# A wait ahead of the position-bias loads of the second attention

## The chip, the cores and the metric

The kernel runs on one core of a Trainium2 chip. The metric is the time of one execution on the device in microseconds. The median of three runs before the change is 2534.94 us (2533.12 to 2541.66).

## The reference

One layer of an encoder is applied to two groups of 2048 tokens (prompt and sample) of width 1024, all in float32. From the normalised input one projection gives queries, keys, values and gates of two attentions. The first attention looks at a window of 128 tokens to either side. The second looks at a neighbourhood: the 2048 tokens are a grid of 32 rows by 64 columns, and each token sees 8 rows by 16 columns around it. Both results are gated, go through one output projection and are added to the input, and a last gated term is added. What matters here is the second attention (cut):

```python
sc = jnp.einsum('bnqhd,banchd->bnhqac', qr, kb).astype(jnp.float32) * scale
drow = rs + jnp.arange(wr) - r + NA_ROWS_MAX - 1
bias = rpb_cols[:, drow].transpose(2, 0, 3, 1, 4)
sc = jnp.where(mask, sc + bias.astype(jnp.float32), -jnp.inf)
...
pr = jax.nn.softmax(sc, axis=-1)
...
o = jnp.einsum('bnqhac,banchd->bnqhd', pr, vb)
```

The bias depends on a head and on where a key lies relative to its query. The kernel reads it, with the mask folded in, from a table in HBM.

## The kernel before, in words

The program has three stages. In the first (up to about 760 us) the first attention runs, in the second (about 760 to 1905 us) the second one, and in the third (from 1905 us) the output projection and the last gate. The change is in the second stage.

The second attention is cut into 64 units, `unit_b(f)`: two halves of the heads, two groups of tokens, and 16 blocks of 8 rows by 16 columns (b counts the four blocks of rows, cb the four of columns, cb fastest). A unit has 128 queries and four heads. Its keys are a window of 12 or 15 grid rows by 24 or 32 columns, so that a head's scores are 128 x 288, 384, 360 or 480. The steps of a unit are:

- `sc(h)`: two matrix products per head make the scores (scb); DVE adds the bias and takes the maximum (`softmax`, L277), and behind the fourth head DVE makes the negative maxima (L288).
- `exps`: ACT makes four exponentials (L294), heads 0, 2, 1, 3 in this order. All but the last units also turn the probabilities into another order: four copies `tn<-s` from one place in SBUF to another, issued by ACT as DMAs between and behind the exponentials (L301). They are pinned to their places in ACT's order.
- `load_values`: SP loads the values (`vw<-v_d`, L891) in three or four pieces into rotating buffers that become free with the products of the unit before.
- `pt(x)`: TensorE transposes a head's copied probabilities (ptb, L262), ACT and DVE split the result into two parts (L923, L924).
- `po(x)`: TensorE multiplies them with the values (pob), and `fin` gates and stores the result (ob_d, L952).

The bias of a unit is loaded by SP (L879) into one of two halves of a buffer `bt[0]`; a unit with cb = 2 has the same table as the one with cb = 1 before it and loads none, so there are 48 loads for 64 units. The load stands in the program at the start of its own unit. It may start as soon as its half of the buffer is free.

The order of TensorE's work is written out: `PLAN_B` says at which share of a unit's time each step is traced, and between the steps the projection of a later unit (pqk and pvg, five to six units ahead) fills TensorE. All its instructions are chained in that order. The other engines' and SP's queues are ordered by a planner, which simulates the program and issues what is ready, earlier instructions of the program first; `P(...)` and `behind(...)` pin single instructions. Within a queue instructions then run strictly in that order. SP's queue in this stage also carries the stores of values (v_d, L837), the loads of the next input (stx, L352), reloads of weights (wa and wb, L197 and L1001) at the two places where the set of weights changes, and loads and stores for later stages.

Of the kernel before, what the change touches and what calls it, by code (L numbers as in the profile page):

```python
# [42 lines left out]
def row_type(b):  # L43
    return (0, 1, 1, 2)[b]


def col_type(cb):
    return (0, 1, 1, 2)[cb]
# [57 lines left out]
def emit(ctx, tc, io):  # L106
    nc = tc.nc
# [37 lines left out]
    copies = []  # L145
# [105 lines left out]
    def behind(ins, other=None):  # L251

        tc.add_manual_dep(ins.ins, (other or last_pe[-1]).name,
                          mybir.DependencyInfo(mybir.DependencyClass.NoSync, mybir.DependencyReason.DATA),
                          reason="behind the product")
# [25 lines left out]
    def sm_tiles():  # L281
        return {"s": [], **{k: ap.tile([128, 4], F32, tag=k, name=k, bufs=3) for k in ("mx", "nm", "den", "rd")}}

    def exps(sm, fct, gs, sink=None, turned=None):

        mx, nm, den, rd, ss = (sm[k] for k in ("mx", "nm", "den", "rd", "s"))
        if sink is None:
            nc.vector.tensor_scalar_mul(nm, mx, -1.0)  # L288
            yield
        else:  # L290
            nc.vector.scalar_tensor_tensor(out=nm, in0=mx, scalar=-1.0, in1=sink[1], op0=ALU.mult, op1=ALU.min)  # L291
        waiting = []
        for n_, i in enumerate((0, 2, 1, 3) if sink is None else range(4)):
            ex = nc.scalar.activation(ss[i], ss[i], AF.Exp, bias=nm[:, i:i + 1], accum_out=den[:, i:i + 1])  # L294
            if sink is None and (n_ == 0 or turned is not None):
                P(ex)
            if sink is None and turned is not None:
                waiting.append(i)
                for k in waiting[:1] if n_ in (1, 2) else waiting[:] if n_ == 3 else ():
                    to = turned[:, k, :ss[k].shape[-1]]  # L300
                    P(nc.scalar.dma_start(to.bitcast(F32), ss[k]))  # L301
                    ss[k] = to
                    waiting.remove(k)
        if sink is not None:
            es = ap.tile([128, 4], F32, tag="es", name="es", bufs=3)
            nc.vector.tensor_tensor(out=es, in0=sink[0], in1=nm, op=ALU.add)
            nc.scalar.activation(es, es, AF.Exp)
            yield
            behind(nc.vector.tensor_tensor(out=den, in0=den, in1=es, op=ALU.add))
            nc.vector.reciprocal(out=nm, in_=den)  # L310
            nc.gpsimd.tensor_copy(rd, nm)
            nc.gpsimd.tensor_copy(rd[0:64, 1::2], nm[64:128, 0::2])
            nc.gpsimd.tensor_copy(rd[64:128, 0::2], nm[0:64, 1::2])
        else:
            nc.vector.reciprocal(out=rd, in_=den)
        nc.gpsimd.tensor_scalar_mul(rd, rd, fct)
        g2 = ap.tile([128, 4, HD], F32, tag="g2", name="g2", bufs=2)
        nc.gpsimd.tensor_tensor(out=g2, in0=gs.rearrange("p (h d) -> p h d", h=4),
                                in1=rd.unsqueeze(2).broadcast_to([128, 4, HD]), op=ALU.mult)
        sm["g2"] = g2.rearrange("p h d -> p (h d)")  # L320
        yield
# [70 lines left out]
    def big(shape, dt, name):  # L392
        return ap.tile(shape, dt, tag="big", name=name, bufs=3)
# [287 lines left out]
    def unit_a(f, kv):  # L681
# [6 lines left out]
        def sc(i):  # L688
            pair, half = divmod(i, 2)
            a, z = span[half]  # L690
            c0, n = 128 * t - 128 + 64 * half, z - a
            if half == 0:
                if not s2:
                    s2.extend([ap.tile([128, 3, 640], F32, tag="ev", name="s2", bufs=1), 0])
                pairs.append(s2[0][:, s2[1] % 3])
                s2[1] += 1
                if not right:
                    nc.gpsimd.memset(pairs[pair][:, 256:320], 0.0)
            ps = ptile([128, 512], "sc", "sc")
            for j, q in enumerate(qs[f]):  # L700
                mm(ps[:, :n], q[kv][:, 128 * i:128 * i + 128], ks_a[:, kv, c0 + a:c0 + z], j == 0, j == 1)
            softmax(i, ps, n, mask[:, a:z], sm, pairs[pair][:, 320 * half + a:320 * half + z])
            if i == 3:
                got["ex"] = exps(sm, y[:, 11:12], gs[:, 256 * kv:256 * kv + 256],
                                 (snk[:, 0, 4 * kv:4 * kv + 4], snk[:, 1, 4 * kv:4 * kv + 4]))
                next(got["ex"])
# [156 lines left out]
    bt = []  # L863

    def unit_b(f):
        half, st = divmod(f - 2 * NT, 2 * NT)
# [6 lines left out]
        n = nr * ncol  # L873
        if cb != 2:
            off, _ = BIAS_OFF[(row_type(b), col_type(cb))]
            if not bt:
                bt.append(big([128, 2, 4, 512], F32, "bias"))
            bt.append(bt[0][:, len(bt) % 2])
            nc.sync.dma_start(bt[-1][:, :, :n], io["bias"][half][:, off:off + 4 * n].rearrange("p (h n) -> p h n", h=4))  # L879
        bias = bt[-1]  # L880
        vw = []

# [18 lines left out]
        def sc(h):  # L901
            ps = ptile([128, 512], "sc", "scb")
            for j, q in enumerate(qs[f]):
                mm(ps[:, :n].rearrange("p (r c) -> p r c", c=ncol), q[h % 2][:, 128 * (h // 2):128 * (h // 2) + 128],
                   ks_b[h % 2][:, r0:r0 + nr, h // 2, c0:c0 + ncol], j == 0, j == 1)
            softmax(h, ps, n, bias[:, h, :n], sm)
            if h == 3:
                if not tn:
                    tn.append(ap.tile([128, 4, 480], F32R, tag="ev", name="tn", bufs=1))
                got["ex"] = exps(sm, hr_b[:, st:st + 1], gs, turned=tn[0] if f < 6 * NT - AHEAD - 1 else None)  # L910
                next(got["ex"])
# [204 lines left out]
    for f in range(6 * NT):  # L1116
# [8 lines left out]
        for kv in range(2 if in_a else 1):  # L1125
            unit = unit_a(f, kv) if in_a else unit_b(f)
            for part, now, act, i in PLAN_A if in_a else PLAN_B:
                at = (kv + part) / (2 if in_a else 1)
                while spent < at * total:
                    spent += next(stream, total)  # L1130
                if now or prev:
                    (unit if now else prev)[act](i)
            prev = unit
# [18 lines left out]
    with tc.tile_pool(name="c", bufs=1, reuse_waits="tile") as op:  # L1152
# [208 lines left out]
        for m in range(7 * len(groups)):  # L1361
            n, i = divmod(m, 7)
# [94 lines left out]
```

## Time and profile before

| what | value |
|---|---|
| median of three runs | 2534.94 us (2533.12 to 2541.66) |
| the profiled execution's own time | 2547.61 us |
| its span, first to last instruction | 2545.8 us |
| TensorE (PE) busy | 2469.8 us, 97% |
| VectorE (DVE) busy | 1704.6 us, 67% |
| ScalarE (ACT) busy | 1413.7 us, 56% |
| GpSimd (POOL) busy | 851.1 us, 33% |
| mean granted TensorE clock | 0.989 |
| loads of the bias (L879) | 48, of 576 to 960 KB |
| copies tn<-s (L301) | 232, of 144 to 240 KB |

PE is TensorE's matrix products, PEld its weight loads, DVE VectorE, ACT ScalarE, POOL GpSimd, SP SyncE. ACTq and SPq are the sequencers of ACT and SP, which issue DMAs. A row of a timeline gives start, duration, engine, line, operation and the names of the tiles (out<-in), with the number of merged instructions; in brackets stands the idle time of the engine before it and what ended that. A row of the windows view gives the stretch, its length, the busy time and number of instructions of each engine (PE, PEld, DVE, ACT, POOL), the granted clock of TensorE as a share of full speed, the busy share of the DMA engines and GB/s. A row of waits gives who waited for whom: us in total, number of times, longest.

### The profile page before, as it was taken

The page shows a single profiled execution, that of the slowest core. Times are in us where ns is not written, and L with a number is a line of the kernel's source. Part 1 is how long each engine was busy: PE and PEld are TensorE (multiplying, and loading weights), DVE is VectorE, ACT ScalarE, POOL GpSimd, SP SyncE. Part 2 cuts the span into 40 slices and gives each one's busy share as a digit, 9 for nine tenths or more (in the row PEclk, how much of TensorE's full clock was granted, in tenths as well). Part 3 has the DMA queues.
Part 4 walks back from the last instruction along what each step waited for, and adds up shares of the span by engine and source line. Part 5 has one row for each costly group of instructions (what it writes and reads, how often), then busy time and mean ns, then how long its engine had stood idle before and what let it go on. Part 6 is the DMA issues. An engine that isn't in the chain of part 4 may idle for free. (4 is left out here: it accounts for less than half of the span.)

```text
span 2545.8 us, 40929 instructions
## 1 busy us (share of the span) xinstructions
PE 2469.8 (97%) x13062; PEld 2073.9 (81%) x13062; DVE 1704.6 (67%) x4215; ACT 1413.7 (56%) x3408; POOL 851.1 (33%) x1363
## 2 busy tenths in 40 slices
PE   8999999999999999999999999999899999999999
PEld 7888888888888777887777777877778888888887
DVE  6877777777765665666566666665545665777776
ACT  5777777767664555565555555665664222344443
POOL 4555555555443544444444333433110000000000
PEclk9999999999999999999999999999999999999999
DMA  6423323232445766666977676776968555656665
GB/s 206 133 92 98 96 92 100 90 100 92 137 139 176 232 211 213 221 228 202 336 228 220 192 240 225 233 242 218 334 205 298 166 182 178 230 181 238 226 227 172
DMA packets 279288, 485.55 MB, mean 191 GB/s; under 512 B 31617, under 2 KB 120097, under 8 KB 274849
## 3 DMA queue, kind: packets, MB, share of 16 engines
q1 hardware_dynamic: 245376, 437.84, 52.6%
q10 hardware_dynamic: 33696, 45.09, 5.0%
q8 instruction: 104, 1.70, 0.3%
q14 instruction: 112, 0.91, 0.1%
HBM read 307.72 MB, written 134.23 MB: 174 GB/s over the span
## 5 line engine op out<-in xcount | busy, mean ns | idle before, releaser
L258 PE MATMUL pqk<-wa,xr 128*128 128x512 f32 x1536 | 464.2, 420 | 0.0
L258 PE MATMUL pvg<-wb,xr 128*128 128x512 f32 x1536 | 449.0, 405 | 0.0
L294 ACT ACTIVATE s<-s,nm 128x320 f32<-128x320 f32 (+6 forms) x512 | 293.4, 574 | 131.7 <-DVE nm L291 118.8
L258 PEld LDWEIGHTS pvg<-wb,xr 128*128 128x128 f32 x1536 | 271.8, 189 | 33.6
L258 PEld LDWEIGHTS pqk<-wa,xr 128*128 128x128 f32 x1536 | 263.6, 193 | 30.3
L370 POOL TENSOR_TENSOR xr<-stx,xr 128x512 fp32r<-128x512 f32 x186 | 238.2, 1292 | 136.2 <-ACT xr L369 103.2
L1242 ACT CAST opd<-raw 128x512 fp32r<-128x512 f32 x224 | 131.5, 618 | 270.6 <-PE acca L1260 117.9
L1243 DVE TENSOR_TENSOR opd<-raw,opd 128x512 fp32r<-128x512 f32 x224 | 146.7, 688 | 145.3 <-ACT opd L1242 145.3
L258 PE MATMUL pg<-wb,xr 128*128 128x512 f32 x768 | 233.1, 410 | 1.0 <-DVE vv L527 1.0
L258 PE MATMUL pq<-wa,xr 128*128 128x512 f32 x768 | 219.4, 400 | 0.0
L924 DVE TENSOR_TENSOR p_t<-ptb,p_t 128x368 fp32r<-128x368 f32 (+5 forms) x256 | 122.8, 488 | 135.7 <-ACT p_t L923 133.9
L942 ACT COPY otb<-pob 64x512 f32<-64x512 f32 x128 | 74.3, 581 | 209.2 <-PE pob L258 208.9
L923 ACT CAST p_t<-ptb 128x368 fp32r<-128x368 f32 (+5 forms) x256 | 107.6, 426 | 138.4 <-PE ptb L262 127.4
L1260 PE MATMUL accc<-opd,wb 128*128 128x512 f32 x768 | 176.7, 390 | 0.0
L1260 PE MATMUL acca<-opd,wa 128*128 128x512 f32 (+1 forms) x780 | 175.9, 386 | 0.5 <-ACT r L1338 0.5
L1260 PE MATMUL acca<-opd,s 128*128 128x512 f32 x768 | 175.4, 390 | 0.0
L143 POOL TENSOR_TENSOR yb<-vrb,power 128x8 f32<-128x8 f32 x64 | 106.4, 1662 | 200.0 <-DVE vrb L804 196.0
L1260 PEld LDWEIGHTS acca<-opd,wa 128*128 128x128 f32 x780 | 145.1, 188 | 30.1 <-ACT r L1338 0.7
L1260 PEld LDWEIGHTS accc<-opd,wb 128*128 128x128 f32 x768 | 144.3, 188 | 29.8
L1260 PEld LDWEIGHTS acca<-opd,s 128*128 128x128 f32 x768 | 144.2, 188 | 29.8
L262 PEld LDWEIGHTS ptb<-rowwise,tn 128*128 128x128 f32 (+2 forms) x756 | 86.6, 140 | 98.6 <-DMA tn<-s 63.9
L258 PEld LDWEIGHTS pob<-p_t,vw 128*128 128x128 f32 (+2 forms) x832 | 135.8, 193 | 27.3 <-DVE p_t L924 7.6
(174 smaller groups left out, 5244.2 us busy)
## 6 DMA issues: line engine op xcount, KB each, us to landing
stx<-x_b SPq DMA_DIRECT2D x128, 256.0 KB
vw<-v_d SPq DMA_DIRECT2D x96, 256.0 KB
stx<-x_a SPq DMA_DIRECT2D x64, 256.0 KB
stn<-x_n SPq DMA_DIRECT2D x64, 256.0 KB
v_d<-vb SPq DMA_DIRECT2D x64, 256.0 KB
ple_d<-ev SPq DMA_DIRECT2D x64, 256.0 KB
xres<-x_r SPq DMA_DIRECT2D x64, 256.0 KB
x_d<-r SPq DMA_DIRECT2D x64, 256.0 KB
```

The costliest lines, as they stand in the source:

```text
L143: nc.gpsimd.tensor_tensor(out=y, in0=v, in1=power.broadcast_to([128, n]), op=ALU.pow)
L258: pinned(nc.tensor.matmul(out, lhsT, rhs, start=start, stop=stop))
L262: pinned(nc.tensor.transpose(out.bitcast(F32R), in_, eye))
L294: ex = nc.scalar.activation(ss[i], ss[i], AF.Exp, bias=nm[:, i:i + 1], accum_out=den[:, i:i + 1])
L370: low.tensor_tensor(out=lo, in0=raw, in1=hi.bitcast(F32), op=ALU.subtract)
L923: nc.scalar.copy(hi, pf)
L924: nc.vector.tensor_tensor(out=lo, in0=pf, in1=hi.bitcast(F32), op=ALU.subtract)
L942: nc.scalar.copy(ot[a:a + 64], pq[z:z + 64])
L1242: P(nc.scalar.copy(hi, v))
L1243: P(nc.vector.tensor_tensor(out=lo, in0=v, in1=hi.bitcast(F32), op=ALU.subtract))
L1260: pinned(nc.tensor.matmul(ps[:, cols], w[k][:, a, c:c + 128], o[:, b, cols], start=i in (0, 1, 4) and k == 0 and j == 0, stop=k == 3 and j ...
```

## The change

The kernel keeps a note of the last exponential of the second attention that was traced, `last_ex`. Each load of a bias gets a dependency on the instruction noted there when the load is traced: SP waits with the load until that exponential has finished. `after` is the helper that enters the dependency. The copies, the exponentials and the sizes of all transfers stay as they are.

```diff
+    last_ex = []
+
+    def after(ins, other):
+
+        tc.add_manual_dep(ins.ins, other.name, mybir.DependencyInfo(mybir.DependencyClass.Sync, mybir.DependencyReason.DATA),
+                          reason="behind the copies")
+
...
             ex = nc.scalar.activation(ss[i], ss[i], AF.Exp, bias=nm[:, i:i + 1], accum_out=den[:, i:i + 1])
+            if sink is None:
+                last_ex[:] = [ex.ins]
...
-            nc.sync.dma_start(bt[-1][:, :, :n], io["bias"][half][:, off:off + 4 * n].rearrange("p (h n) -> p h n", h=4))
+            load = nc.sync.dma_start(bt[-1][:, :, :n],
+                                     io["bias"][half][:, off:off + 4 * n].rearrange("p (h n) -> p h n", h=4))
+            if last_ex:
+                after(load, last_ex[0])
```

## The prediction

> **What bounds the kernel now.** I read the page first, then the waits of the stretch in which the second attention runs, then busy times unit by unit, then the queues.
>
> ```profile
> span 2545.8 us, 40929 instructions
> PE 2469.8 (97%) x13062; PEld 2073.9 (81%) x13062; DVE 1704.6 (67%) x4215; ACT 1413.7 (56%) x3408; POOL 851.1 (33%) x1363
> ```
>
> TensorE (PE) is busy for 97% of the span, so only its idle 76 us and its slow stretches can be won. The waits from 807 to 1800 us (who waited for whom: us in total, times, longest), the last two rows from other queues:
>
> ```profile
> PE ptb L262 <- DMA tn<-s: 44.9, 46, 2.8
> PE pob L258 <- DVE p_t L924: 2.3, 5, 0.9
> ACT q1b L857 <- DMA bias<-bias: 6.9, 3, 2.3
> SPq L879 <- DVE nm L288: 60.3, 14, 6.3
> ```
>
> PE's one large wait is for the copies tn<-s, by which the exponentials of a unit get into the order that its transposes (ptb) read. Now stretches of the windows view, each from a unit's first exponential to the next one's: length, then the busy times of PE, PEld, DVE, ACT, POOL, then PE's granted clock. The first and third units (cb=1) have no bias load in them; the second and fourth, the next ones (cb=2) with the same shapes, have one:
>
> ```profile
> 1035.25:1051.13 15.88, 15.88 (x88) 13.24 (x87) 10.49 (x27) 9.66 (x23) 7.94 (x9) 1.00 0.70 232
> 1051.13:1067.69 16.56, 15.52 (x88) 12.86 (x87) 10.37 (x27) 9.71 (x23) 6.67 (x8) 1.00 0.76 251
> 1166.84:1183.67 16.83, 16.83 (x96) 14.15 (x95) 11.24 (x27) 9.96 (x23) 7.93 (x9) 1.00 0.52 165
> 1183.67:1201.98 18.31, 16.78 (x96) 13.83 (x95) 10.74 (x27) 10.15 (x23) 7.98 (x9) 1.00 0.81 263
> ```
>
> Without a load PE is never idle; with one the unit is 0.7 to 1.5 us longer, all of it idle PE. The reason stands in the queues. SP's timeline, ACT's, then PE's, for those first two units and the one before them:
>
> ```profile
> 1018.75 0.38 SPq L879 DMA_DIRECT2D bias<-bias  x1
> 1019.22 0.93 SPq L891 DMA_DIRECT2D vw<-v_d  x2
> ...
> 1034.46 1.28 SPq L891 DMA_DIRECT2D vw<-v_d  x3
> ...
> 1050.35 1.28 SPq L891 DMA_DIRECT2D vw<-v_d  x3
> 1051.72 0.38 SPq L879 DMA_DIRECT2D bias<-bias  x1
> ```
>
> ```profile
> 1035.99 0.47 ACTq L301 DMA_DIRECT2D tn<-s  x1
> ...
> 1051.87 0.47 ACTq L301 DMA_DIRECT2D tn<-s  x1
> ...
> 1053.05 0.62 ACT L294 ACTIVATE s<-s,nm 128x384 f32<-128x384 f32 x1
> ...
> 1053.80 1.22 ACTq L301 DMA_DIRECT2D tn<-s  x1
> ```
>
> ```profile
> 1025.31 0.35 PE L262 MATMUL ptb<-rowwise,tn 128*96 128x128 f32 x3
> ...
> 1041.00 0.45 PE L262 MATMUL ptb<-rowwise,tn 128*128 128x128 f32 x3
> ...
> 1044.02 0.46 PE L258 MATMUL pob<-p_t,vw 128*128 128x256 f32 x3
> 1044.83 0.38 PE L262 MATMUL ptb<-rowwise,tn 128*128 128x128 f32 x3
> ...
> 1058.02 0.45 PE L262 MATMUL ptb<-rowwise,tn 128*128 128x128 f32 x3 [1.04 <-DMA tn<-s]
> ```
>
> In the unit without a load the first copy is issued at 1035.99 and PE reads it at 1041.00, 5.0 us later, without waiting. In the next one a bias load goes out 0.15 us ahead of the first copy (1051.72, 1051.87), and the copy is there after 6.15 us: PE stood for 1.04. In the unit before both the load went out at 1018.75, well ahead of the exponentials, and the first transposes at 1025.31 waited for nothing. So the load hurts when it starts among the copies. Their sizes, of the units with 384 and 480 columns and of the load shared by most:
>
> ```profile
> tn<-s ACTq DMA_DIRECT2D x60, 240.0 KB
> bias<-bias SPq DMA_DIRECT2D x16, 720.0 KB
> ...
> tn<-s ACTq DMA_DIRECT2D x56, 192.0 KB
> ```
>
> The stall has a second price. After many of these stalls the granted clock is 0.50 for 3.4 us. Ten such stretches lie in units with a load and a stall (the first and the last are shown, then the 3.4 us just ahead of the one at 992.0, and the whole stage):
>
> ```profile
> 937.40:940.80 3.40, 3.40 (x13) 2.71 (x13) 0.92 (x2) 1.05 (x3) 1.73 (x2) 0.50 0.71 237
> ...
> 1749.80:1753.20 3.40, 3.40 (x15) 2.86 (x14) 0.54 (x1) 0.98 (x2) 2.12 (x2) 0.50 0.27 77
> 988.60:992.00 3.40, 1.92 (x12) 1.45 (x13) 1.75 (x4) 1.95 (x5) 0.40 (x1) 1.00 1.08 383
> ...
> 810.77:1799.61 988.84, 938.06 (x5040) 772.05 (x5038) 618.70 (x1562) 567.72 (x1335) 422.74 (x491) 0.98 0.71 230
> ```
>
> **The change part by part.** No instruction goes or comes but a semaphore wait ahead of 47 of the 48 bias loads (the first has no exponential before it). What is waited for is more than it seems. A load is traced when its own unit begins, and the exponential then on record is the fourth of the unit before. Today a load goes out as soon as its half of the double buffer is free, that is behind the last softmax of the unit that read it (the 60.3 us in which SP stands at L879 for DVE nm), one to three units ahead of use. Afterwards it goes out one unit ahead, behind that unit's fourth exponential: in the second unit shown at about 1053.05 + 0.62, near 1053.8 in place of 1051.72, 2.1 us later, and level with the fourth copy.
>
> *Stalls at ptb, 44.9 us.* The copies' first three are then issued 0.7 to 1.9 us ahead of the load, as in a unit with none. The fourth goes out beside it, 1053.80 - 1051.13 = 2.65 us behind the first exponential. Taking for it the 6.15 us of the copy that had a load 0.15 us ahead, it lands at 2.65 + 6.15 = 8.8, and PE asks for it at 1044.83 - 1035.25 = 9.6: covered by 0.8 us. So the units with a load become like those without. Bounds: all 44.9 gone, or 20 left if the fourth copy misses by half a us in most units. I take 40, near the upper end, since the row without a load (PE busy 15.88 of 15.88) is the nearest case; the rest is kept for stalls that have another cause.
>
> *Clock.* Ten stretches at half clock cost 10 x 3.4 x 0.5 = 17 us; the whole stage's row says 988.84 x (1 - 0.98) = 20. Each lies in a unit whose stall is 1.5 us or longer. I take 17; bounds 8 (if half the stalls stay) and 20.
>
> *ACT's wait on a landing.* In units whose load leads, ACT stood up to 2.3 us at its fourth copy until the bias had landed (6.9 in 3 waits), and PE behind that 2.3 us at pob. With the load behind the copies this goes: 1 us, bounds 0 and 2.3.
>
> *A load that comes too late.* DVE adds the bias to a unit's four score products. The rows that tell how long a load takes, when it is needed, and SP's queue where weights are reloaded (one piece of the chain of waits, DVE's and SP's timeline):
>
> ```profile
> 1620.30 5.08 DMA bias<-bias
> 1047.90 0.55 DVE L277 CUSTOM_DVE_ANT_0 s<-scb,bias 128x384 f32<-128x384 f32 x1
> ...
> 1221.57 5.86 SPq L197 DMA_DIRECT2D wa<-sp_1wa  x5
> 1227.66 1.87 SPq L891 DMA_DIRECT2D vw<-v_d  x2
> 1229.58 0.43 SPq L879 DMA_DIRECT2D bias<-bias  x1
> ...
> 1234.88 0.64 DVE L277 CUSTOM_DVE_ANT_0 s<-scb,bias 128x480 f32<-128x480 f32 x1
> 1786.03 0.44 SPq L879 DMA_DIRECT2D bias<-bias  x1
> ...
> 1789.89 0.64 DVE L277 CUSTOM_DVE_ANT_0 s<-scb,bias 128x480 f32<-128x480 f32 x1
> ```
>
> In an ordinary unit a load issued at 2.65 behind the first exponential is needed at 1047.90 - 1035.25 = 12.65, 10.0 us later, and takes 5.08 in a quiet case; beside copies I estimate 7.5 (the 6.15 of a 192 KB copy and some 500 KB more at the 383 GB/s of the window at 988.60). It is hidden, with 2.5 us to spare. Not so at the two reloads of weights: the load at 1229.58 is not for the softmax at 1234.88 but two units on; the load for that softmax was issued a unit earlier. It will now queue with the weights in SP, most likely at that same place, and land 5.08 to 7.5 us later: 0 to 2.2 us late; at 1786.03, 1.2 to 3.6 us late. If it is put ahead of the weights it costs nothing. Bounds 0 and 5.8; I take 4, near the upper end, since the weights share its way.
>
> *The wait itself* holds SP from the load's turn to the exponential. Behind it stand the store of ob_d, then v_d and the next x, which go out 1.5 us and more later anyway; ACT, DVE and PE execute nothing more.
>
> Sum: 40 + 17 + 1 - 4 = 54 us. Against the profiled execution's own 2547.6 (span 2545.8) that gives 2493.6. That execution is 12.7 us above the median of the runs shown, 2534.94. The last 640 us are free of such waits, so the surplus probably lies in these same stalls; then a timed run has only 54 - 12.7 = 41 to win. Between 41 and 54 I take 48: **2487 us**.
>
> **The rivals.**
>
> *The collision only moves.* The load still goes out level with the fourth copy and 0.65 us behind the third. For it: the 0.8 us of cover is thin, and wider units have copies of 240 KB instead of 192, so 6.15 may be 7.7 there. If half the units with a load lose 1 us at their last transposes and half the slow clock stays, 54 falls by 21 + 8.5 to 25: 2510 us. Against: PE asks for the four copies 1.1 to 1.5 us apart (1041.00 to 1044.83), and they are issued 0.65 apart, so each later copy has more room.
>
> [...]
>
> *The clock stays slow.* If something else than these stalls halves the clock, the 17 us stay: 2504. For it: the window 988.60 to 992.00 ahead of a slow one was no idle one, PE was busy in 1.92 of its 3.40 us. Against: all ten lie in units with a long stall.
>
> [...]
>
> *SP stands in the way (slower).* If the planner leaves the load ahead of the value loads vw, as at 1018.75 and 1019.22 now, these wait for the fourth exponential too. vw would go from 1050.35 to 1053.8 and behind 720 KB, 3.4 + 2 us later. Without that, vw issued by 1035.74 is used by pob at 1044.02, 8.3 us later, of which it needs 5.08 to 7.5; so a unit would lose 2.2 to 4.6, say 3.4 us. It decides from 17 units on (17 x 3.4 = 58, what the rest wins); in all 42 it makes 2535 - 48 + 143 = 2630, in half of them 2558. Against: today's lead comes where the softmax ends before vw's buffer is free; the fourth exponential ends 3 us later, when at 1050.35 vw has been issued in the common order.
>
> *Given back elsewhere (no change).* The bytes stay, and the DMA engines are busy 0.71 of the stage. 2 us later the load meets v_d's store and the next x, whose split PE needs. If that stall is as long, 2535. Against: the unit of 1166.84 has room (0.52), and x is issued late in a unit for the next but one.
>
> **How the numbers follow.** Forecast 0.60, clock stays slow 0.05, collision moved 0.15, no change 0.09, SP in the way 0.11. About 0.3% (7.6 us) is what a measurement of this kernel can tell from no change: faster 0.60 + 0.05 + 0.15 = 0.80, same 0.09, slower 0.11. The forecast's own range: 44.9 + 20 + 2.3 = 67 less nothing gives 2468; 20 less of stalls and 9 less of clock leaves 25, 2510. The range that leaves out the slower case and most of no change is 2468 to 2520.
>
> **What would show it.** Right: PE's wait at ptb for tn<-s falls from 44.9 to below 8; the clock of the stage is 1.00; outside the reloads every bias load starts 2.4 to 3.5 us behind its unit's first exponential; units of 1051.13's and 1183.67's kind take 15.9 and 16.8. DVE waits for the bias at the two reloads, by up to 5.8 us together. Wrong: pob waiting for vw (SP in the way), waits at the third and fourth ptb of a unit (collision moved), DVE waiting for the bias in ordinary units, or PE waiting for xr.

## The result and the profile after

The changed kernel takes 2491.13 us (median of four runs, 2490.16 to 2493.02) where the one before takes 2536.16 us (2533.12 to 2541.66) beside it: a ratio of 0.9821, with a 95% interval of 0.9802 to 0.9840. That is 45 us faster. The forecast was 2487 us and 48 us. The change shifts the line numbers: the exponentials are L301 now, the copies L310, the loads of the bias L888, the loads of the values L903, the store of ob_d L964.

The head of the page:

```profile
span 2490.3 us, 40934 instructions
...
PE 2447.5 (98%) x13062; PEld 2060.5 (83%) x13062; DVE 1705.6 (68%) x4215; ACT 1412.8 (57%) x3408; POOL 853.1 (34%) x1363
```

The span is 55.5 us shorter than that of the profiled execution before. TensorE's idle time, the span less its busy time, went from 2545.8 - 2469.8 = 76.0 to 42.8 us: 33 us. Its busy time for the same 13062 products went from 2469.8 to 2447.5: 22 us, which is mostly the clock (its mean went from 0.989 to 0.998, and 0.009 of 2500 us is 23). The waits of the stage (from 807 us to the last copies):

```profile
PE ptb L262 <- DMA tn<-s: 15.8, 18, 3.1
...
PE scb L258 <- DVE mx L277: 3.6, 2, 2.5
DVE s L277 <- DMA bias<-bias: 3.0, 2, 2.1
...
PE pob L258 <- DVE p_t L936: 0.4, 2, 0.2
```

TensorE's wait for the copies fell from 44.9 to 15.8 us. ACT's wait for a bias to land (6.9 us) has no row left. New are the two rows in the middle: VectorE waits for a bias, and TensorE behind it. Now the four kinds of units that the prediction showed, two without a load and, behind each, one with a load and the same shapes; then the whole stage, one reload of weights and the stretch at half clock within it:

```profile
1020.34:1035.96 15.62, 15.62 (x88) 13.25 (x87) 10.50 (x27) 9.77 (x23) 7.96 (x9) 1.00 0.71 236
1035.96:1051.28 15.32, 15.32 (x88) 12.89 (x87) 10.10 (x27) 9.64 (x24) 6.71 (x8) 1.00 0.85 271
1145.52:1162.32 16.80, 16.80 (x96) 14.13 (x95) 11.27 (x27) 9.97 (x24) 7.96 (x9) 1.00 0.53 165
1162.32:1179.44 17.12, 16.56 (x96) 13.88 (x95) 10.84 (x27) 9.97 (x24) 7.98 (x9) 1.00 0.87 280
810.07:1768.00 957.93, 935.74 (x5137) 777.46 (x5136) 630.81 (x1589) 580.58 (x1367) 426.82 (x498) 1.00 0.76 245
1196.54:1218.73 22.19, 18.04 (x88) 14.43 (x87) 11.05 (x27) 9.86 (x24) 7.89 (x9) 0.92 0.92 307
1205.50:1208.90 3.40, 3.40 (x13) 2.72 (x13) 1.68 (x4) 1.89 (x4) 2.91 (x2) 0.50 1.00 352
```

The narrow unit with a load took 16.56 us before and takes 15.32 now, with no idle TensorE. The wide one (480 columns) went from 18.31 to 17.12 and still holds 0.56 us of idle time, a wait for a copy at its first transposes:

```profile
1168.72 0.54 PE L262 MATMUL ptb<-rowwise,tn 128*128 128x128 f32 x4 [0.56 <-DMA tn<-s]
```

The queues of the narrow unit, SP, ACT, then the transposes on TensorE:

```profile
1035.18 1.28 SPq L903 DMA_DIRECT2D vw<-v_d  x3
1037.96 0.37 SPq L964 DMA_DIRECT2D ob_d<-o_tb  x1
1038.61 0.38 SPq L888 DMA_DIRECT2D bias<-bias  x1
```

```profile
1036.70 0.47 ACTq L310 DMA_DIRECT2D tn<-s  x1
...
1038.61 0.83 ACTq L310 DMA_DIRECT2D tn<-s  x1
```

```profile
1041.64 0.37 PE L262 MATMUL ptb<-rowwise,tn 128*128 128x128 f32 x3
...
1045.38 0.38 PE L262 MATMUL ptb<-rowwise,tn 128*128 128x128 f32 x3
```

The load goes out at 1038.61, level with the fourth copy and 1.9 us behind the first, and behind all three pieces of the values. None of the four transposes waits, the fourth one neither. At a reload of weights it looks different. SP's queue there:

```profile
1199.01 7.13 SPq L197 DMA_DIRECT2D wa<-sp_1wa  x5
1206.22 0.38 SPq L888 DMA_DIRECT2D bias<-bias  x1
```

And VectorE, then TensorE (in square brackets the wait ahead of the instruction and what ended it):

```profile
1215.89 0.66 DVE L277 CUSTOM_DVE_ANT_0 s<-scb,bias 128x480 f32<-128x480 f32 x1 [0.93 <-DMA bias<-bias]
```

```profile
1216.61 0.49 PE L258 MATMUL scb<-ks_b,q1b 128*128 128x480 f32 x1 [1.05 <-DVE mx L277]
```

The load stands behind five loads of weights in SP's queue. It has landed 9.7 us after its issue (1206.22 to 1215.89), and the softmax of the next unit waits for it.

### The profile page after: what moved, and what is told of

The parts are those of the page before. It is cut to its first block, busy times and chain, and to the rows that moved or that the text cites. A ratio compares the mean times of both kernels' runs of the same rounds, so it can differ in the third digit from the quotient of the medians.

```text
span 2490.3 us, 40934 instructions
## 1 busy us (share of the span) xinstructions
PE 2447.5 (98%) x13062; PEld 2060.5 (83%) x13062; DVE 1705.6 (68%) x4215; ACT 1412.8 (57%) x3408; POOL 853.1 (34%) x1363
## 5 line engine op out<-in xcount | busy, mean ns | idle before, releaser
L258 PE MATMUL pqk<-wa,xr 128*128 128x512 f32 x1536 | 452.5, 411 | 0.0
L301 ACT ACTIVATE s<-s,nm 128x320 f32<-128x320 f32 (+6 forms) x512 | 293.5, 575 | 131.1 <-DVE nm L298 119.1
L258 PEld LDWEIGHTS pqk<-wa,xr 128*128 128x128 f32 x1536 | 257.1, 188 | 29.7
L258 PEld LDWEIGHTS pq<-wa,xr 128*128 128x128 f32 x768 | 135.1, 189 | 17.3
```

The source lines that it names most:

```text
L258: pinned(nc.tensor.matmul(out, lhsT, rhs, start=start, stop=stop))
```

## The experiments

**Theory.** A load hurts when its bytes run beside the copies that TensorE needs next. **Rivals.** The gain comes from SP's queue, where the load no longer stands for the softmax with the value loads behind it, or from the planner's other order; or what hurts is a further DMA in between, whatever its size. Each time below is a median, each ratio is against the kernel before on the same chip with its 95% interval, and each diff is against the changed kernel.

**1. The load waits for the first exponential in place of the fourth.**

```diff
-            if sink is None:
+            if sink is None and n_ == 0:
                 last_ex[:] = [ex.ins]
```

> Each load waits for the first exponential of the unit before its own in place of the fourth; all else is as in the changed kernel, also the load's coming one unit ahead of use and behind the value loads in SP's queue. Theory (a load hurts when its transfer runs among the copies): it goes out at 0.7 to 1.0 us behind the first exponential, the first transposes wait 1 to 2 us again in most of the 43 units with a load, the clock halves again about ten times; 2520 to 2545 us. Rival (the gain comes from SP's queue, which no longer stands at the load for the softmax with the value loads behind it, or from the planner's other order): 2488 to 2500 us.

Measured: 2535.48 us, ratio 1.0002 (0.9986 to 1.0018): the whole gain is gone. The narrow unit of this kernel on SP, on ACT and on TensorE, and then the waits of the stage:

```profile
1049.05 1.28 SPq L903 DMA_DIRECT2D vw<-v_d  x3
1050.57 0.39 SPq L888 DMA_DIRECT2D bias<-bias  x1
```

```profile
1050.57 0.47 ACTq L310 DMA_DIRECT2D tn<-s  x1
```

```profile
1056.30 0.45 PE L262 MATMUL ptb<-rowwise,tn 128*128 128x128 f32 x3 [0.60 <-DMA tn<-s]
```

```profile
PE ptb L262 <- DMA tn<-s: 41.0, 53, 2.6
```

The load still comes one unit ahead, and in this unit it still stands behind the values, as in the changed kernel; its start moved by 2 us, to a place ahead of the store of ob_d. Elsewhere the order in SP's queue is not the same: in 25 of the 42 units with a load the last piece of the values now goes out behind the load. TensorE's waits of this run have no row for late values; what came back is its waits for the copies, and with them the slower clock (a mean of 0.994 in its ten executions, 0.997 in eight of the changed kernel). Whether the bytes or the orders of the queues make these waits, this run cannot tell by itself; run 9, with the same start and nearly the same order, can. One thing was not as expected: in the profiled execution the clock is at half in four stretches of the stage, not in about ten.

**2. The load waits for the fourth exponential of the unit that frees its half of the buffer.** `last_ex` keeps one entry per unit.

```diff
-            if sink is None:
-                last_ex[:] = [ex.ins]
+            if sink is None and n_ == 0:
+                last_ex.append(ex.ins)
+            elif sink is None:
+                last_ex[-1] = ex.ins
...
-            if last_ex:
-                after(load, last_ex[0])
+            loaded_by.append(f - 2 * NT)
+            if len(loaded_by) > 2:
+                after(load, last_ex[loaded_by[-2] - 1])
```

> Each load waits for the fourth exponential of the unit that frees its half of the buffer, so it is still behind the copies of that unit but one to three units ahead of use, as before the change. Theory (the wait of 3 us at the two reloads of weights, and what follows from it, comes from the load's going out one unit ahead): DVE no longer waits for the bias there, 3 to 9 us less than the changed kernel: 2482 to 2488 us. Rival (the reloads are slow by themselves): 2489 to 2493 us.

Measured: 2487.03 us, ratio 0.9810 (0.9780 to 0.9840); again, as run 8 below, 2484.76 us, 0.9787 (0.9767 to 0.9807).

**3. No loads but the first two.**

```diff
-            load = nc.sync.dma_start(bt[-1][:, :, :n],
...
+            if len(bt) <= 3:
+                nc.sync.dma_start(bt[-1], io["bias"][half][:, off:off + 2048].rearrange("p (h n) -> p h n", h=4))
```

> All loads but the first two are left out, so later units add a wrong bias; nothing else is left out. It gives what the loads still cost in the changed kernel. Theory (the stalls that are left, 16 us at the transposes, are mostly the loads': the fourth copy, and the two reloads): 2470 to 2480 us. Rival (what is left comes from other transfers, above all the value loads that run into the copies in units with four pieces): 2482 to 2490 us.

Measured: 2479.17 us, ratio 0.9777 (0.9747 to 0.9808). By the medians the loads still cost some 11 us in the changed kernel (run 4); the two intervals overlap by a little.

**4. The changed kernel again, beside these.**

> The changed kernel again, for comparison on the same chip. Every theory: 2488 to 2495 us.

Measured: 2490.49 us, ratio 0.9828 (0.9792 to 0.9864). The waits on TensorE and for a bias, of run 2, of run 3 and of this one:

```profile
PE ptb L262 <- DMA tn<-s: 12.3, 21, 1.4
```

```profile
PE ptb L262 <- DMA tn<-s: 9.1, 9, 2.0
```

```profile
PE ptb L262 <- DMA tn<-s: 7.1, 14, 1.4
PE scb L258 <- DVE mx L277: 6.6, 2, 3.5
...
DVE s L277 <- DMA bias<-bias: 3.0, 1, 3.0
```

Two things follow. First, with the loads one to three units ahead again no engine waits for a bias, and the row of scb (6.6 us here, 3.6 in the other execution) is gone: the wait at the reloads does come from the load's lateness. The times say the same, 3.5 us less, but their intervals overlap; the waits carry it. Second, without any load TensorE still waits 9.1 us for copies, and the changed kernel's own two executions show 15.8 and 7.1. So much of what is left at the transposes is not the bias's. The time of run 3 lies in the range of its theory, yet at the transposes its rival was right: what is left there comes mostly from other transfers.

**5. The load waits for the third exponential.**

```diff
-            if sink is None:
+            if sink is None and n_ <= 2:
                 last_ex[:] = [ex.ins]
```

> Each load waits for the third exponential of the unit before, so it goes out some 2.0 us behind the first one, 0.65 us sooner than in the changed kernel and level with the third copy. Theory (what counts is how many copies are on their way ahead of the load; each is asked for 1.0 to 1.5 us after the one before): two copies are safely ahead, the third and fourth share with the load and mostly have time; some waits at the third transposes come back: 2490 to 2505 us. Rival (only a load behind the last exponential helps): 2510 to 2540 us.

Measured: 2491.56 us, ratio 0.9812 (0.9791 to 0.9833), as the changed kernel. The waits:

```profile
PE ptb L262 <- DMA tn<-s: 8.3, 15, 0.9
PE scb L258 <- DVE mx L277: 6.5, 2, 3.9
DVE s L277 <- DMA bias<-bias: 5.9, 2, 3.8
```

But the edit moved the load by less than was meant. SP's queue and the third copy in the narrow unit of this run:

```profile
1039.88 0.37 SPq L964 DMA_DIRECT2D ob_d<-o_tb  x1
1040.36 0.58 SPq L888 DMA_DIRECT2D bias<-bias  x1
```

```profile
1039.89 0.51 ACTq L310 DMA_DIRECT2D tn<-s  x1
```

The store of ob_d stands ahead of the load, and the load goes out 0.47 us behind the third copy. In units of every width it is issued about 2.5 us behind the first exponential, where the changed kernel has 2.5 to 2.9. So three copies are still on their way ahead of it, the load came as a rule at most 0.4 us sooner, and an equal time is what either idea would give. Whether two copies ahead are enough is not shown.

**6. As run 2, and the fourth piece of the values waits for the last exponential of its own unit.** **7. The third piece too, in units with four.** **10. The third piece in all units.** Run 7's part beside run 2's:

```diff
-                nc.sync.dma_start(v[:kn[j]].bitcast(F32).rearrange("p h d -> p (h d)"),
+                got_v = nc.sync.dma_start(v[:kn[j]].bitcast(F32).rearrange("p h d -> p (h d)"),
...
+                if nch == 4 and j > 1:
+                    after(got_v, last_ex[-1])
```

In run 6 the condition is `j == 3`, in run 10 it is `j > 1`.

> As the second experiment (the load waits for the unit that frees its half), and the fourth piece of the values, where a unit has four, waits for the last exponential of its own unit, so that it no longer runs among the copies. Theory (the stalls that are left in the wide units with 480 columns, 0.6 to 1.6 us each in about nine units and there without any load too, are the fourth piece's): PE's wait at the transposes falls from 12.3 to 4 to 8 us; 2478 to 2484 us. Rival (the piece then comes too late for the products, or was not the cause): 2485 to 2495 us.

> As the run before it, with the third and the fourth piece of the values held back. Theory: no better at the transposes than with the fourth alone, and the products of some units wait for the values, which are issued 2.7 to 3.6 us behind the first exponential and needed at 8.8: 2478 to 2492 us. Rival (every piece ahead of the copies costs): 2472 to 2478 us.

> The second experiment again, for comparison on the same chip. Every theory: 2482 to 2490 us.

> As the seventh experiment (loads behind the copies of the unit that frees their half, third and fourth piece of the values behind the copies), with the third piece held back in the units with three pieces as well. Theory (these units have no stall at the transposes to win; their products ask for the values at 8.5, 6 us behind the held piece): 2473 to 2480 us, the same. Rival (the piece comes too late there): 2482 to 2500 us.

Measured: run 6 2479.99 us, ratio 0.9766 (0.9745 to 0.9787); run 7 2475.34 us, 0.9752 (0.9731 to 0.9773); run 8 2484.76 us, 0.9787 (0.9767 to 0.9807); run 10 2479.61 us, 0.9776 (0.9761 to 0.9790). The waits at the transposes of run 6:

```profile
PE ptb L262 <- DMA tn<-s: 7.1, 11, 1.6
```

The same wide unit on TensorE, and then the waits, of run 7:

```profile
1165.47 0.46 PE L262 MATMUL ptb<-rowwise,tn 128*128 128x128 f32 x4
```

```profile
PE ptb L262 <- DMA tn<-s: 3.5, 9, 0.6
...
PE pob L258 <- DMA vw<-v_d: 1.6, 2, 1.2
```

The waits of run 10:

```profile
PE pob L258 <- DMA vw<-v_d: 5.8, 6, 1.7
PE ptb L262 <- DMA tn<-s: 2.4, 6, 0.6
```

The wide unit's first transposes wait no more, where they waited for 0.56 us in the changed kernel and, without any load of a bias, for 0.68:

```profile
1169.98 0.54 PE L262 MATMUL ptb<-rowwise,tn 128*128 128x128 f32 x4 [0.68 <-DMA tn<-s]
```

So the stall left in the wide units was the values', and the fourth piece is enough to make it: in run 6, which holds back that piece alone, no wide unit outside the reloads waits at its first transposes any more. Run 7 did better than its theory at the transposes (3.5 us), its wait for late values is small, and its time lies in the range of its rival, by which every piece ahead of the copies costs. (In its wide units the second piece, too, went out behind the copies, although nothing holds it but its place in SP's queue.) Run 10 shows where that turns: TensorE's wait for values rises from 1.6 to 5.8 us, against 1.1 us won at the copies. Run 7 has the lowest median of all and, by its interval (at most 0.9773), is faster than the changed kernel (at least 0.9802). The intervals of runs 6, 7, 8 and 10 all overlap; among them the waits decide, not the times.

**9. As run 1, with a quarter of the bytes.** The first two loads are whole; after that only one head's bias is loaded.

```diff
+            else:
+                load = nc.sync.dma_start(bt[-1][:, :1, :n], io["bias"][half][:, off:off + n].rearrange("p (h n) -> p h n", h=1))
```

> As the first experiment (the load goes out among the copies), but every load after the first two brings the bias of one head of four, a quarter of the bytes; the other heads add an old bias, so the output is wrong. Theory (the load's bytes share the DMA engines with the copies): the stalls fall with the bytes, to 5 to 15 us at the transposes: 2480 to 2500 us. Rival (what hurts is that another DMA is issued and handled at all between the copies, whatever its size): 2520 to 2540 us.

Measured: 2486.51 us, ratio 0.9807 (0.9790 to 0.9824), with this wait for the copies:

```profile
PE ptb L262 <- DMA tn<-s: 15.6, 19, 2.1
```

A load at the worst moment with a quarter of its bytes costs nothing measurable over a whole one at a good moment. The load starts as early as in run 1 (0.7 us behind the first exponential), and the last piece of the values goes out behind it in 24 of 43 units, in run 1 in 25 of 42. So neither the early start as such, nor one more DMA, nor the order in SP's queue makes the waits of run 1 (41.0 us there, 15.6 here): it is the load's size. Whether its bytes count or the number of its packets was not told apart.

## Why the prediction was right, point by point

- **Direction and mechanism: right.** The wait moves the load behind the first three copies, the narrow units with a load become like those without, and outside the reloads nothing takes the stall's place. Experiment 1 takes away the lead of the copies and with it all of the gain (2535.48 us); experiment 9 gives the gain back by the load's size alone (2486.51 us).
- **Size: right, in part by luck.** 48 us was a choice between 41 and 54, and 45 was measured. In the profiled executions the four terms came out as 29 + 15 + 2 - 4 = 42 us where the sum has 40 + 17 + 1 - 4 = 54. The spans differ by 55.5 all the same, since about 8 us of clock outside the stage and 4 us of idle time behind 1800 us (12.3 before, 7.9 after) went as well; both were in no term, and no run shows that they come from the change.
- **Stalls at ptb, 40 us: too high.** 44.9 fell to 15.8, so 29 us; in the second execution of the same kernel to 7.1, so 38. The sign of being right, below 8, came in one of the two. The step that was off is "since the row without a load (PE busy 15.88 of 15.88) is the nearest case". It holds for the narrow units. Two other places keep their stalls. Of the 15.8 us, 9.5 lie in six units around the two reloads of weights (1.7 in the second execution), which the prediction left out of this term. Another 5.2 us lie at the first transposes of six wide units elsewhere. In a wide unit without a load three pieces of the values are issued, the last 0.3 us ahead of the first copy; in the unit behind it there are four, up to the moment of the first copy, and the fourth, not the bias, makes the 0.56 us that is left there (runs 3, 6 and 7). That units of 1183.67's kind would take 16.8 us was wrong for this reason: 17.12. (A slip in the working changes nothing: 1053.80 - 1051.13 is 2.67, not 2.65.)
- **The fourth copy, 0.8 us to spare: right in the main.** No wait at the fourth transposes in the unit shown, and outside the reloads 0.6 us in three units, 2.6 us with the reloads. So the rival by which the collision only moves came to under 1 us there. In these runs a load among the copies slows them by its size: a quarter of the bytes takes the stalls from 41.0 us (run 1) to 15.6 (run 9). But the fourth copy, issued level with the load, is mostly there in time, as TensorE asks for it only 6.8 us later (1038.61 to 1045.38).
- **Clock, 17 us: right for this stage of the profiled execution, too high for the timed runs.** The clock of the stage rose from 0.98 to 1.00: eleven stretches at half clock became two, both at reloads, which is 15 us. The rival by which the clock stays slow did not come. That the profiled execution's surplus of 12.7 us would not be there to win in timed runs was right. Its place was not: the surplus is the clock's as a whole (0.989 against a mean of 0.994 in the 31 timed executions of that kernel beside the experiments, 0.005 x 2546 = 13 us), and some 8 of the 28 us lost to the clock lie outside these stalls, in the first 25 us of the program and behind 1800 us.
- **The load that comes too late, 4 us: right.** The load went to the place behind the weights, as foreseen, and TensorE lost 3.6 us in one execution and 6.6 in the other; the second is above the upper bound of 5.8. Run 2 takes it away.
- **ACT's wait on a landing, 1 us: right within its bounds of 0 and 2.3.** TensorE's wait for p_t at pob fell from 2.3 to 0.4 us, so 1.9.
- **SP in the way: did not come.** In every unit of the stage outside the reloads the unit's values are issued ahead of the bias (1035.18 and 1038.61 in the unit shown).

What the 45 us of the timed runs are made of can be estimated. TensorE's idle time fell by 33 us, and by 36 in the second profiled execution of the changed kernel (span 2486.4, busy 2446.8). The mean clock was 0.994 in 31 timed executions of the kernel before and 0.997 in eight of the changed one: 0.003 x 2500 = 8 us. Together that is 41 to 44.

## What to carry to other kernels

Where an engine waits for a small transfer, look at what large transfer starts beside it and how much slack that one has; making the large one wait for the last producer of the small ones costs a semaphore and here won 1.8%. Compare units of equal shape that differ in that transfer alone: they give the price before anything is built. Then choose, among the events behind the small transfers, one that still leaves the large transfer its lead (run 2 chose one to three units ahead), and look at the places where its queue is crowded (here the reloads), for there a short lead was not enough: the load landed 9.7 us after its issue, and TensorE lost 3.6 us in one execution and 6.6 in the other. Last, read from the trace whether the transfer really moved as the wait was meant to move it: in run 5 another DMA of the same queue stood ahead of it.

## What was not expected of the hardware

In these runs the clock's loss does not follow the stalls closely. The kernel before, and experiment 1, in the view of spans and mean granted clocks, with the row of the changed kernel between them:

```profile
core 0: 2545.8 us, clock 0.989
```

```profile
core 0: 2490.3 us, clock 0.998
```

```profile
core 0: 2529.2 us, clock 0.996
```

Experiment 1 has 41.0 us of stalls at the transposes and the kernel before 44.9, yet the lost clock is 2529.2 x 0.004 = 10 us in the one and 2545.8 x 0.011 = 28 us in the other; the 18 us between them are about the 16.6 between the two spans, while the medians of the two kernels are the same. Part of this loss is not the stalls': in the first 25 us of the program the granted clock is 0.80 in the kernel before and 0.86 in experiment 1. But in the stage itself, too, eleven stretches at half clock (19 us lost) stand against four (7 us). So beside nearly the same stalls 7 us of clock were lost in one execution and 19 in another, and the profiled execution of the kernel before was a costly one: its 31 timed executions beside the experiments have clocks of 0.991 to 0.997, with a mean of 0.994, which is also the mean of the ten of experiment 1. Nor does the longer stall decide in the two units compared: in the kernel before, TensorE was idle for 1.53 us in the unit from 928.07 and the clock halved in it, for 2.07 us in the unit from 909.20 and it did not. Nor was TensorE idle throughout ahead of every slow stretch: it was busy for 1.92 of the 3.40 us from 988.60 to 992.00 in the kernel before, and for the 3.40 us behind them the granted clock was 0.50. What makes the clock halve was not tried.
